# The first phase of a decoder block on one core: x by token halves, the first scaled half on VectorE, squares four tiles at a time

## The chip, the core and the metric

The kernel runs on one core of a Trainium2 chip. TensorE (PE) multiplies, VectorE (DVE), ScalarE (ACT) and GpSimd (POOL) do elementwise work, SyncE (SP) issues loads; each engine takes its instructions in its own order, and semaphores order the engines against each other. The metric is the device time in microseconds of one execution; the median of several runs is given.

## The reference

One layer of a decoder block over 512 tokens of 1024 channels, in float32:

```python
h = rmsnorm(x, norm1_g)
proj = h @ w_in            # columns: conv mixer, q, k and v of three branches, gates
y_a = a_b * causal_dwconv(a_c * a_x, conv_a_w)
y_b = nsa(q, compressed, selected and window keys, gates)
x = x + (gm_a * (y_a @ w_a_out) + gm_b * (y_b @ w_b_out)) @ w_o
h = rmsnorm(x, norm2_g)
x = x + (silu(causal_dwconv(h @ w_g) + b) * (h @ w_u)) @ w_down
```

where `rmsnorm(x, g) = x * rsqrt(mean(x*x) + eps) * g`. For this case only the first norm and the first part of `h @ w_in` matter: the 1048 token columns (q, keys, values, gates).

## The kernel before

x lies transposed in memory, as 8 tiles of 128 channels by 512 tokens (`KD` = 8). A float32 product is made of three products of a faster 32-bit format: a number is split into a high part `h` (a cast on ACT) and a rest `l` (a subtraction on DVE), and TensorE adds up h·h, h·l and l·h. The factor `rsqrt(mean(x*x))` of a token is a scale of a whole row, so it is left out of the products and applied when a result is read from its bank. x is only multiplied by the channel's gain `g`: `scale_x` makes `xg_h` (ACT) and `xg_l` (DVE).

The first phase (`tok_round`) makes the 1048 token columns of tokens 0 to 255 (two groups of 128, the tiles `pj_s`, `pj_t` and `pj_o`, six banks). It runs over k = 0 to 7. For each k, `on_k` scales x, loads the weight tile `wr_t` of k (512 KB), splits it (`wh_t` by ACT, `tok_lo` by DVE; the eight rests are kept for later), and adds the squares of x to `sq_sum` (a square on ACT, `square_x`, and an addition on DVE). TensorE then runs 18 products. x arrives in six loads of one or two whole tiles, in buffers of the tag `w4`, which all short-lived tiles of this phase share.

At k = 5 (`ROT_AT`) the tables of the rotary embedding are begun (`rotary_tables`), small steps on DVE, with two functions of ACT that each need a table load.

Behind the eight tiles, `row_scales` sums `sq_sum` over channels by eight short products into `pr`, and DVE (`ms`) and POOL (`r_n`) make the row factor of each token. `compress_in(0)` is a product of all of x with one weight tile (`wh_kc`, `wl_kc`, into `pkc`, 24 products of 512 columns). Then `tok_keep` casts weight tiles k = 0 to 3 again and keeps them (`th`, four buffers of the tag `th`), `compress_in(1)` is a second such product, and `tok_round_lag` makes the token columns of tokens 256 to 511, with the kept weights first and then with k = 4 to 7 loaded anew (`wr_t`, the first of them called t24 here). It writes to the same banks as the first phase, so it waits for `evac`: ACT reads three banks `pj_s` with the row factor, DVE the other three.

All raw weights, of the first phase, of `compress_in`, `tok_keep` and of the second round, go through three buffers of the tag `wr` (`NWR`), the split ones through two (`wh`). The order on each engine, and which buffer a tile gets, is chosen by the scheduler that builds the program; `behind` ties an instruction behind another by hand.

```python
raw = sb.tile([P, TOKC], F32, name=f"wr_th{k}", tag="wr", bufs=NWR)
h = th.tile([P, TOKC], F32R, name=f"th{k}", tag="th", bufs=LAG)
```

Of the kernel before, what the change touches and what calls it, by code (L numbers as in the profile page):

```python
# [11 lines left out]
F32 = mybir.dt.float32  # L12
F32R = mybir.dt.float32r
I32 = mybir.dt.int32
AF = mybir.ActivationFunctionType
ALU = mybir.AluOpType
AX = mybir.AxisListType

P = 128
D = 1024  # L20
S = 512
KD = D // P
# [20 lines left out]
TOKC = C_G + 24  # L43
# [5 lines left out]
ROT_AT = 5  # L49
LAG = 4  # L50

X_AT = {1: 1, 2: 2, 4: 2, 6: 1}
NWU = 9
QT_ORDER = (3, 2, 1, 0)
NPT = 3
NF_T = 10
# [13 lines left out]
CH = ((0, 350), (350, 700), (700, TOKC))  # L70

G1, G2, CAW, FCW, FCB = 0, 8, 16, 28, 94
# [17 lines left out]
def tile_block(ctx: ExitStack, tc: tile.TileContext, xT, pos, par, par2, w_tok, w_a3, w_gate, w_ao, w_bo, w_o,  # L90
               w_ff, w_dn, c_w1, out):
    nc = tc.nc
# [3 lines left out]
    pa = in_ctx.enter_context(tc.tile_pool(name="pa", bufs=1, side="left"))  # L96
    at_ctx = ExitStack()
    pb = at_ctx.enter_context(tc.tile_pool(name="pb", bufs=1, side="right"))
    pr_ctx = ExitStack()
    pp = pr_ctx.enter_context(tc.tile_pool(name="pp", bufs=1, side="right"))  # L100

    def const(shape, name, dt=F32, pool=sb):
        return pool.tile(shape, dt, name=name, tag=name)

    def w_tmp(name, shape):

        t = pp.tile([P, TOKC], F32, name=name, tag="w4", bufs=NW4)
        v = t[:, :math.prod(shape)]
        if len(shape) == 2:
            v = v.rearrange("p (a b) -> p a b", a=shape[0])  # L110
        elif len(shape) == 3:
            v = v.rearrange("p (a b c) -> p a b c", a=shape[0], b=shape[1])
        return v
# [4 lines left out]
    def d_bank(name):  # L118
        return bank("d", name, 2)
# [11 lines left out]
    loads, splits = [], []  # L131
# [30 lines left out]
    wu = d_bank("wu")  # L162
    for i in range(NWU):
        nc.tensor.matmul(wu[:, 0:P], ones, ones, start=True, stop=True)
    par_sb = const([P, NPAR], "par")
    xg_h = const([P, KD, S], "xg_h", F32R, pa)
    xg_l = const([P, KD, S], "xg_l", F32R, pa)
    sq_sum = w_tmp("sq_sum", (S,))


    def tok_banks(tt):
# [22 lines left out]
    def tok_round(tts, on_k):  # L194
        banks = [tok_banks(tt) for tt in tts]
        for k in range(KD):
            wh, wl = on_k(k, lambda first=0: load_w(w_tok[k], TOKC, f"t{tts[0]}{k}", first=first, mid=k > 0, lo=tok_lo_of(k)))
            for tt, bank in zip(tts, banks):
                tok_products(tt, bank, k, [wh[:, a:b] for a, b in CH], wl, k == 0, k == KD - 1)
        return banks  # L200
# [23 lines left out]
            tok_products(t1, banks[1], k, [kept[k][:, a:b] for a, b in CH], tok_lo_of(k), False, k == lag - 1)  # L224
        return banks

    def scale_x(k, xr, c):
        g = par_sb[:, G1 + k:G1 + k + 1]
        hi = nc.scalar.activation(xg_h[:, k, c], xr[:, c], AF.Copy, scale=g)
        nc.vector.scalar_tensor_tensor(xg_l[:, k, c], xr[:, c], g, xg_h[:, k, c].bitcast(F32),  # L230
                                       op0=ALU.mult, op1=ALU.subtract)
        return hi

    def square_x(k, xr, after):
        sq = sq_sum if k == 0 else w_tmp(f"sq{k}", (S,))
        behind(nc.scalar.activation(sq, xr, AF.Square), after)
        if k > 0:
            nc.vector.tensor_add(sq_sum, sq_sum, sq)

    xrs = {}  # L240

    def load_x(k, n):
        t = w_tmp(f"xr{k}", (n, S))
        for i in range(n):
            xrs[k + i] = t[:, i]
        nc.sync.dma_start(t, xT[:, k:k + n])

    def behind(later, earlier):

        tc.add_manual_dep(later.ins, earlier.ins.name,  # L250
                          mybir.DependencyInfo(mybir.DependencyClass.NoSync, mybir.DependencyReason.DATA),
                          reason="order")

    def on_k(k, load):
        if k == 0:

            load_x(0, 1)
            nc.sync.dma_start(par_sb, par)
            first, rest = slice(0, S // 2), slice(S // 2, S)
            scale_x(0, xrs[0], first)  # L260
            w = load(CH[0][1])
            load_x(1, 1)
            hi = scale_x(0, xrs[0], rest)
        else:
            hi = scale_x(k, xrs[k], slice(0, S))
            w = load(CH[0][1] if k == 1 else 0)
            if k in X_AT:
                load_x(k + 1, X_AT[k])
        square_x(k, xrs[k], splits[-1] if k < 2 else hi)
        if k == ROT_AT:  # L270

            for d in (nc.sync.dma_start(pos_i, pos), nc.sync.dma_start(par2_sb, par2)):
                behind(d, loads[-1])
            rotary_tables()
        return w


# [9 lines left out]
    def rotary_tables():  # L287
# [22 lines left out]
        for i, gi in enumerate((0, 2, 3)):  # L310
# [5 lines left out]
            nc.vector.tensor_tensor(tsin[:, i, :, HALF:], sn, glo, op=ALU.mult)  # L316

    banks0, banks1 = tok_round((0, 1), on_k)

    ident = const([P, P], "ident")  # L320
# [382 lines left out]
            nc.vector.scalar_tensor_tensor(mix_a[j], mix_a[j], 1.0, acc, op0=ALU.add, op1=ALU.mult)  # L703


    th_ctx = ExitStack()
    th = th_ctx.enter_context(tc.tile_pool(name="th", bufs=1, side="left"))
    compress_in(0)
    kept = [tok_keep(k) for k in range(2)]
    compress_in(1)  # L710
# [43 lines left out]
    half = D // 2  # L754
# [86 lines left out]
    for i in range(4):  # L841
# [6 lines left out]
        w = load_w(w_bo[i], D, f"bo{i}")  # L848
        for n, j in enumerate((2 * i, 2 * i + 1)):
# [7 lines left out]
                                           op0=ALU.mult, op1=ALU.subtract)  # L857
# [37 lines left out]
    for n, j in enumerate(order):  # L895
        w = load_w(w_o[j], D, f"o{j}")
# [6 lines left out]
        sq = sq2 if n == 0 else pc.tile([P, S], F32, name=f"sqb{j}", tag="tb", bufs=3)  # L903
# [208 lines left out]
```

## Time and profile before

| What | Value |
|---|---|
| median of 3 runs | 729.7 us (729.38 to 730.1) |
| span of the profiled execution, first to last instruction | 728.6 us |
| PE busy | 722.1 us, 99% |
| ACT busy | 416.8 us, 57% |
| bytes moved | 90.36 MB, 124 GB/s in the mean |
| granted clock of TensorE | 1.000 |

The profiled execution is recorded by its span, 728.6 us; a time of its own is not given, and the runs beside it are the three of the first row. In the profile, a row of the order of time has the start in us, the duration in us, the engine, the line, the operation, the tiles (written from read) and the count; in brackets stands how long the engine had been idle and what ended that. A row of a stage (a window) gives the length, then for PE, PE's weight load, DVE, ACT and POOL the busy time with the count, the granted clock, the share of the load engines and GB/s. PE's durations are modelled and overlap: the distance of two starts is what a product costs. Names in the profile lack the numbers of tiles.

### The profile page before, as it was taken

What the parts mean: (1) busy time and instruction counts of PE and PEld (TensorE: products, weight loads), DVE (VectorE), ACT (ScalarE), POOL (GpSimd) and SP (SyncE); (2) the same over time, 40 slices, a digit from 0 to 9 for tenths busy, and PEclk for the clock granted to TensorE, in tenths of its full rate; (3) what the DMA queues carried; (4) which work ended last, traced back from release to release, by engine and by line L of the source; (5) the groups of instructions that cost most, each with busy time, mean ns of one, the idle gap of its engine ahead of it and who ended that gap; (6) DMA issues with size and microseconds to landing.
All of it is one profiled execution on the core that took longest, in us unless ns stands there. A gap on an engine that the chain in (4) does not pass through costs nothing.

```text
span 728.6 us, 11253 instructions
## 1 busy us (share of the span) xinstructions
PE 722.1 (99%) x4315; PEld 641.7 (88%) x4315; DVE 568.2 (78%) x979; ACT 416.8 (57%) x697; POOL 122.7 (17%) x113
## 2 busy tenths in 40 slices
PE   8999999999999999999999999999999999999997
PEld 8999878888888888778889999999999999999986
DVE  6986966667556676688876989999898988989833
ACT  6866556758666676544666565555545564545320
POOL 2020334333333210322002010001000000000000
PEclk9999999999999999999999999999999999999999
DMA  8753551112111221245544686544655546552403
GB/s 289 243 167 109 150 140 60 57 62 83 58 59 58 75 70 58 72 160 173 195 138 107 142 186 165 159 127 115 152 141 142 145 117 155 135 144 88 117 29 116
DMA packets 36309, 90.36 MB, mean 124 GB/s; under 512 B 7456, under 2 KB 9120, under 8 KB 36256
## 3 DMA queue, kind: packets, MB, share of 16 engines
q1 hardware_dynamic: 30320, 76.75, 33.0%
q0 software_dynamic: 5648, 12.58, 10.4%
q8 instruction: 34, 0.56, 0.3%
q10 hardware_dynamic: 288, 0.31, 0.1%
q14 instruction: 19, 0.16, 0.1%
HBM read 87.54 MB, written 2.10 MB: 123 GB/s over the span
## 4 chain that ended last, share of the span: by engine, by line
PE 95%; DMA 3%; ACT 1%; DVE 0%; issue 0%; POOL 0%; SPq 0%; POOLq 0%
PE p L376 10%; PE p L372 10%; PE p L369 10%; PE pdn L369 4%; PE pdn L372 4%; PE pdn L376 4%; PE pg L369 4%; PE pg L374 4%; PE pg L372 4%; PE pa L369 3%; PE pa L372 3%; PE pt L623 2%; PE po L369 2%; PE po L372 2%; PE po L376 2%; PE pa L376 2%
## 5 line engine op out<-in xcount | busy, mean ns | idle before, releaser
L369 PE MATMUL p<-xf_h,sh 128*128 128x256 f32 x352 | 87.4, 281 | 0.0
L372 PE MATMUL p<-xf_l,sh 128*128 128x256 f32 x352 | 87.2, 281 | 0.0
L369 PEld LDWEIGHTS p<-xf_h,sh 128*128 128x128 f32 x352 | 66.3, 188 | 0.1
L372 PEld LDWEIGHTS p<-xf_l,sh 128*128 128x128 f32 x352 | 66.3, 188 | 0.0
L376 PE MATMUL p<-xf_h,sl 128*128 128x256 f32 x352 | 55.8, 281 | 0.0
L781 POOL DMA_DIRECT2D wl_d<-in_w_dn_dram x16 | 19.1, 1195 | 210.6 <-ACT wl_d L780 210.6
L758 ACT ACTIVATE sh<-s 128x1024 fp32r<-128x1024 f32 x44 | 45.8, 1051 | 15.1 <-DVE s L798 8.1
L759 DVE TENSOR_TENSOR sl<-s,sh 128x1024 fp32r<-128x1024 f32 x44 | 53.1, 1216 | 1.3 <-ACT sh L758 1.2
L372 PE MATMUL pdn<-al,wh_d 128*128 128x512 f32 x134 | 52.6, 393 | 0.0
L369 PE MATMUL pdn<-ah,wh_d 128*128 128x512 f32 x134 | 52.3, 392 | 0.0
L369 PE MATMUL pg<-xg_h,wh_g 128*128 128x512 f32 x128 | 51.0, 398 | 0.0
L372 PE MATMUL pg<-xg_l,wh_g 128*128 128x512 f32 x128 | 50.8, 397 | 0.0
L374 PE MATMUL pg<-xg_h,wl_g 128*128 128x512 f32 x128 | 50.7, 396 | 0.0
L376 PEld LDWEIGHTS p<-xf_h,sl 128*128 128x128 f32 x352 | 47.8, 188 | 0.2
L369 PE MATMUL p<-xf_h,wh_s 128*128 128x256 f32 x176 | 43.7, 281 | 0.0
L372 PE MATMUL p<-xf_l,wh_s 128*128 128x256 f32 x176 | 43.7, 281 | 0.0
L596 ACT ACTIVATE e<-sc,mx 128x256 f32<-128x256 f32 (+3 forms) x64 | 33.2, 524 | 13.0 <-DVE mx L595 11.6
L369 PE MATMUL pa<-xg_h,wh_a 128*128 128x512 f32 x96 | 38.5, 401 | 0.0
L372 PE MATMUL pa<-xg_l,wh_a 128*128 128x512 f32 x96 | 37.9, 395 | 0.0
L627 DVE TENSOR_TENSOR pl<-pt,ph 128x512 fp32r<-128x512 f32 x40 | 26.9, 683 | 13.7 <-ACT ph L626 13.6
L758 ACT ACTIVATE th<-wr_s 128x512 fp32r<-128x512 f32 x20 | 12.7, 634 | 39.5 <-issue 28.4
L600 ACT ACTIVATE e<-e,sums 128x512 f32<-128x512 f32 (+3 forms) x64 | 30.8, 552 | 7.6 <-DVE sums L574 7.6
(330 smaller groups left out, 2132.2 us busy)
## 6 DMA issues: line engine op xcount, KB each, us to landing
wr_s<-in_w_ff_dram SPq DMA_DIRECT2D x44, 512.0 KB, 3.5
wr_d<-in_w_dn_dram SPq DMA_DIRECT2D x22, 512.0 KB, 3.7
wr_g<-in_w_gate_dram SPq DMA_DIRECT2D x16, 512.0 KB, 3.4
wl_d<-in_w_dn_dram POOLq DMA_DIRECT2D x16, 512.0 KB, 6.4
wr_a<-in_w_a_dram SPq DMA_DIRECT2D x12, 512.0 KB, 3.5
wr_t<-in_w_tok_dram SPq DMA_DIRECT2D x10, 524.0 KB, 5.1
wr_o<-in_w_o_dram SPq DMA_DIRECT2D x8, 512.0 KB, 3.6
wr_th<-in_w_tok_dram SPq DMA_DIRECT2D x4, 524.0 KB, 3.9
```

What stands on the lines that cost most here:

```text
L369: m = nc.tensor.matmul(acc, wh, xh, start=first and i == 0, stop=False)
L372: nc.tensor.matmul(acc, wh, xl, start=False, stop=False)
L374: m = nc.tensor.matmul(acc, wl, xh, start=False, stop=last and i == n - 1)
L376: m = nc.tensor.matmul(acc, wl, xh, start=False, stop=last and i == n - 1)
L596: nc.scalar.activation(e[:, i, 0:nk], sc[:, o:o + nk], AF.Exp, bias=mx[:, i], accum_out=sums[:, i])
L600: nc.scalar.activation(v, v, AF.Copy, scale=sums[:, i])
L623: ends["pt"] = nc.tensor.transpose(pt[:, i * P:(i + 1) * P], e[:, i, kt * P:(kt + 1) * P], ident)
L627: nc.vector.tensor_sub(pl, pt, ph.bitcast(F32))
L758: nc.scalar.activation(h, v, AF.Copy)
L759: nc.vector.tensor_sub(l, v, h.bitcast(F32))
L781: nc.gpsimd.dma_start(view(l), src, accum_op=ALU.add)
```

## The change

x is loaded by token halves (`XH` = 256): tokens 0 to 255, which alone the first phase multiplies, in five loads that begin with single tiles, and tokens 256 to 511 in two loads of four tiles at k = 5 and k = 6. The halves lie in four tiles of the tag `th`, whose pool is opened earlier for it; the kept weights use the same four buffers afterwards. The very first scaled half is made by VectorE. The second half is scaled at k = 6 and 7. Squares are taken of four tiles of a half at once (1024 columns on ACT), and DVE adds the four by one reduction with a stride, so there are four squares, four reductions and two additions of 256 columns, where there were eight squares and seven additions of 512. `sq_sum` has a buffer of its own. The parameters come in two loads, and one of nine warming products is left out.

```diff
-X_AT = {1: 1, 2: 2, 4: 2, 6: 1}
-NWU = 9
+XH = 256
+NWU = 8
...
-    sq_sum = w_tmp("sq_sum", (S,))
+    sq_sum = const([P, S], "sq_sum", F32, pp)
...
-    def square_x(k, xr, after):
-        sq = sq_sum if k == 0 else w_tmp(f"sq{k}", (S,))
-        behind(nc.scalar.activation(sq, xr, AF.Square), after)
-        if k > 0:
-            nc.vector.tensor_add(sq_sum, sq_sum, sq)
...
+    def x_tile(half, q):
+        t = th.tile([P, TOKC], F32, name=f"xr{half}{q}", tag="th", bufs=LAG)
+        xrs[half, q] = t[:, 0:4 * XH].rearrange("p (k t) -> p k t", k=4)
+
+    def load_x(half, k, n):
+        if k % 4 == 0:
+            x_tile(half, k // 4)
+        return nc.sync.dma_start(xrs[half, k // 4][:, k % 4:k % 4 + n], xT[:, k:k + n, half * XH:(half + 1) * XH])
+
+    def scale_x(half, k, by_dve=False):
...
+        if by_dve:
+            hi = nc.vector.tensor_scalar(xg_h[:, k, c], xr, g, None, op0=ALU.mult)
+        else:
+            hi = nc.scalar.activation(xg_h[:, k, c], xr, AF.Copy, scale=g)
+        nc.vector.scalar_tensor_tensor(xg_l[:, k, c], xr, g, xg_h[:, k, c].bitcast(F32),
+                                       op0=ALU.mult, op1=ALU.subtract)
+        return hi
+
+    def square_x(half, q, after):
+        sq = w_tmp(f"sq{half}{q}", (4, XH))
+        behind(nc.scalar.activation(sq, xrs[half, q], AF.Square), after)
+        c = sq_sum[:, half * XH:(half + 1) * XH]
+        if q == 0:
+            nc.vector.tensor_reduce(c, sq.rearrange("p k t -> p t k"), axis=AX.X, op=ALU.add)
+        else:
+            part = w_tmp(f"sqp{half}", (XH,))
+            nc.vector.tensor_reduce(part, sq.rearrange("p k t -> p t k"), axis=AX.X, op=ALU.add)
+            nc.vector.tensor_add(c, c, part)
+
     def on_k(k, load):
         if k == 0:
...
+            load_x(0, 0, 1)
+            nc.sync.dma_start(par_sb[:, 0:CAW], par[:, 0:CAW])
+        hi = scale_x(0, k, by_dve=k == 0)
+        w = load(CH[0][1] if k < 2 else 0)
+        if k == 0:
+            load_x(0, 1, 1)
+        elif k == 1:
+            load_x(0, 2, 2)
+        elif k == 2:
+            load_x(0, 4, 4)
+        elif k == 3:
+            behind(nc.sync.dma_start(par_sb[:, CAW:], par[:, CAW:]), loads[-1])
+        elif k == 4:
+            square_x(0, 0, splits[-1])
         if k == ROT_AT:
...
+            behind(load_x(1, 0, 4), loads[-1])
             rotary_tables()
+        elif k == 6:
+            square_x(0, 1, splits[-1])
+            behind(load_x(1, 4, 4), loads[-1])
+            for j in range(4):
+                behind(scale_x(1, j), splits[-1])
+        elif k == 7:
+            square_x(1, 0, splits[-1])
+            square_x(1, 1, splits[-1])
+            for j in range(4, KD):
+                behind(scale_x(1, j), splits[-1])
         return w
```

What the scheduler makes of it, at the three places of which the prediction speaks. First, ACT around the end of the first phase, before the change (`wh_kc` is the cast for `compress_in`, `th` a kept weight, `qkv` the reading of a bank `pj_s`, `wh_t24` the cast of weight k = 4 of the second round):

```order
L147 ACTIVATE wh_kc0_431<-wr_kc0_430 128x1024
L208 ACTIVATE th0_472<-wr_th0_471 128x1048
L304 ACT_TABLE_LOAD
...
L208 ACTIVATE th1_476<-wr_th1_475 128x1048
L492 ACTIVATE qkv0_528<-pj_s00_95,r_n1_406 128x350
L492 ACTIVATE qkv0_528<-pj_s01_96,r_n1_406 128x350
L492 ACTIVATE qkv0_528<-pj_s02_97,r_n1_406 128x348
L147 ACTIVATE wh_kc1_480<-wr_kc1_479 128x1024
L505 ACTIVATE gate_n_422<-qkv0_528 128x24
L208 ACTIVATE th2_521<-wr_th2_520 128x1048
```

And the same place on ACT after the change:

```order
L149 ACTIVATE wh_kc0_437<-wr_kc0_436 128x1024
L210 ACTIVATE th0_478<-wr_th0_477 128x1048
L331 ACT_TABLE_LOAD
...
L210 ACTIVATE th1_482<-wr_th1_481 128x1048
L333 ACT_TABLE_LOAD
L333 ACTIVATE warm_75<-n_t_260 128x1
L149 ACTIVATE wh_kc1_486<-wr_kc1_485 128x1024
L210 ACTIVATE th2_527<-wr_th2_526 128x1048
L210 ACTIVATE th3_531<-wr_th3_530 128x1048
L149 ACTIVATE wh_t24_665<-wr_t24_664 128x1048
L519 ACTIVATE qkv0_534<-pj_s00_97,r_n1_415 128x350
```

The reading of the first bank stood behind the cast of th1; it stands behind the casts of kc1, th2, th3 and t24 now.

Second, SP's loads from th1 on with the semaphores that each waits for, before the change (DMAHW are earlier loads, DVE and Activation the engine that frees the buffer):

```order
L207 DMA wr_th1_475<-in_w_tok_dram 128x1048 [waits DMAHW6_49,DMAHW2_49,DVE_49]
L146 DMA wr_kc1_479<-in_w_a3_dram 128x1024 [waits DMAHW7_49,DMAHW5_49,Activation_49]
L207 DMA wr_th2_520<-in_w_tok_dram 128x1048 [waits DMAHW4_49,DMAHW0_49,DVE_49]
L207 DMA wr_th3_524<-in_w_tok_dram 128x1048 [waits DMAHW6_49,Activation_49]
L146 DMA wr_t24_658<-in_w_tok_dram 128x1048 [waits DMAHW0_49,Activation_49]
```

And after it:

```order
L209 DMA wr_th1_481<-in_w_tok_dram 128x1048 [waits DMAHW7_49,DMAHW4_49,DVE_49]
L148 DMA wr_kc1_485<-in_w_a3_dram 128x1024 [waits DMAHW6_49,DMAHW0_49,Activation_49]
L209 DMA wr_th2_526<-in_w_tok_dram 128x1048 [waits DMAHW7_49,DMAHW1_49,Activation_49]
L209 DMA wr_th3_530<-in_w_tok_dram 128x1048 [waits DMAHW5_49,DVE_49]
L148 DMA wr_t24_664<-in_w_tok_dram 128x1048 [waits DMAHW3_49,DMAHW1_49,Activation_49]
```

The order of the loads is the same, the buffers are not: th2 had the buffer of kc0 (freed by DVE's `wl_kc`) and has that of th1 now (freed by ACT's cast of th1); th3 has that of kc0. t24 has the buffer of th2 in both.

Third, DVE from its last weight tile of the phase to `wl_kc`, before (`ang` and `n_t` belong to the rotary table):

```order
L155 TENSOR_TENSOR tok_lo3_90<-wr_t07_352,wh_t07_353 128x1048
L299 SCALAR_TENSOR_TENSOR ang_273<-n_t_274,ang_273 128x128
L155 TENSOR_TENSOR wl_kc0_432<-wr_kc0_430,wh_kc0_431 128x1024
L300 TENSOR_SCALAR ang_273<-ang_273 128x128
L347 TENSOR_SCALAR ms_n1_404<-pr_n1_399 128x4
```

And after:

```order
L157 TENSOR_TENSOR tok_lo3_92<-wr_t07_348,wh_t07_349 128x1048
L264 TENSOR_REDUCE sq_sum_88<-sq10_353 128x256
L330 SCALAR_TENSOR_TENSOR n_t_260<-ang_259 128x128
L267 TENSOR_REDUCE sqp1_358<-sq11_356 128x256
L255 SCALAR_TENSOR_TENSOR xg_l_87<-xr11_318,par_85,xg_h_86 128x256 x4
L157 TENSOR_TENSOR wl_kc0_438<-wr_kc0_436,wh_kc0_437 128x1024
L268 TENSOR_TENSOR sq_sum_88<-sq_sum_88,sqp1_358 128x256
```

Between them stand now the two reductions and the four rests of the second half of x. On TensorE the row sums come in two pieces, of two token groups each, the second one behind all but two of the products `pkc`; the second round begins behind `pkc` in both programs.

More of the change, by code (lines that the diff above doesn't have):

```diff
@@ L98, in tile_block @@
     pb = at_ctx.enter_context(tc.tile_pool(name="pb", bufs=1, side="right"))
+    th_ctx = ExitStack()
+    th = th_ctx.enter_context(tc.tile_pool(name="th", bufs=1, side="left"))
     pr_ctx = ExitStack()
@@ L225, in tok_round_lag @@
         return banks
[L227 to L232, printed above, removed]
-    def square_x(k, xr, after):
-        sq = sq_sum if k == 0 else w_tmp(f"sq{k}", (S,))
-        behind(nc.scalar.activation(sq, xr, AF.Square), after)
-        if k > 0:
[L238 to L246, printed above, removed]
     def behind(later, earlier):
@@ L252, in behind @@
                           reason="order")
+    xrs = {}
+    def x_tile(half, q):
[6 more added lines that the diff above has]
+    def scale_x(half, k, by_dve=False):
+        g = par_sb[:, G1 + k:G1 + k + 1]
+        xr = xrs[half, k // 4][:, k % 4]
+        c = slice(half * XH, (half + 1) * XH)
+        if by_dve:
[5 more added lines that the diff above has]
+        return hi
@@ L254, in on_k @@
     def on_k(k, load):
         if k == 0:
[L257 to L269, printed above, removed]
+            load_x(0, 0, 1)
@@ L703, in mix_a_pair @@
             nc.vector.scalar_tensor_tensor(mix_a[j], mix_a[j], 1.0, acc, op0=ALU.add, op1=ALU.mult)
-    th_ctx = ExitStack()
-    th = th_ctx.enter_context(tc.tile_pool(name="th", bufs=1, side="left"))
     compress_in(0)
```

## The prediction

> **What bounds the kernel now.** I read the busy shares first, then the stages, then the waits of TensorE, and last the order of time on ACT, DVE and SP in the first 45 us, since the change lies there.
>
> ```profile
> PE 722.1 (99%) x4315; PEld 641.7 (88%) x4315; DVE 568.2 (78%) x979; ACT 416.8 (57%) x697; POOL 122.7 (17%) x113
> PE 95%; DMA 3%; ACT 1%; DVE 0%; issue 0%; POOL 0%; SPq 0%; POOLq 0%
> 73.00:243.00 170.00, 170.00 (x838) 140.83 (x837) 114.33 (x277) 111.84 (x241) 61.53 (x45) 1.00 0.28 81
> 243.00:390.00 147.00, 146.70 (x718) 121.56 (x717) 113.04 (x217) 87.88 (x176) 24.99 (x22) 1.00 0.36 117
> 390.00:715.00 325.00, 324.53 (x2296) 304.11 (x2295) 278.90 (x369) 165.20 (x202) 24.74 (x23) 1.00 0.51 131
> PE p L376 <- DMA wl_s<-in_w_ff_dram: 0.5, 1, 0.5
> PE ptc L616 <- DVE xs L613: 0.3, 1, 0.3
> ```
>
> TensorE sets the time: the chain is 95% PE, and from 73 us to 715 us it stands still for 0.8 us in all (two waits, which are the last two rows). So a stage behind the first one has no slack in which a delay could vanish, and a microsecond won or lost early arrives whole at the end. What counts is only when TensorE passes the last point that the change moves. TensorE's rows in the first phase, and its way out of it:
>
> ```profile
> 5.66 0.43 PE L186 MATMUL pj_s<-wh_t,xg_h 128*128 128x350 f32 x1 [0.50 <-ACT xg_h L229]
> 11.97 0.64 PE L186 MATMUL pj_s<-wh_t,xg_h 128*128 128x350 f32 x3
> 15.82 0.75 PE L186 MATMUL pj_s<-wh_t,xg_h 128*128 128x350 f32 x3 [0.56 <-ACT xg_h L229]
> 18.84 0.32 PE L186 MATMUL pj_s<-wh_t,xg_h 128*128 128x350 f32 x1
> 21.73 0.64 PE L186 MATMUL pj_s<-wh_t,xg_h 128*128 128x350 f32 x3
> 31.93 0.39 PE L374 MATMUL pkc<-xg_h,wl_kc 128*128 128x512 f32 x1
> 37.02 0.32 PE L186 MATMUL pj_s<-th,xg_h 128*128 128x350 f32 x1
> ```
>
> A channel tile is 18 products; the undisturbed one (k=4) takes 21.73 - 18.84 = 2.89 us. The one at k=2 takes 15.82 - 11.97 = 3.85, so 0.96 us is lost there to late x tiles. Phase two begins at 37.02, where the first product with a kept weight (th) writes bank s of the first round. That bank has to be emptied by ACT first. I measure the change at this instruction: behind it the two programs run the same work, in nearly the same order.
>
> **What emptied the bank in time.** ACT, SP and DVE around it:
>
> ```profile
> 28.61 1.08 ACT L208 ACTIVATE th<-wr_th 128x1048 fp32r<-128x1048 f32 x1 [0.15 <-DMA wr_th<-in_w_tok_dram]
> 33.03 1.07 ACT L208 ACTIVATE th<-wr_th 128x1048 fp32r<-128x1048 f32 x1
> 34.00 1.42 ACT L492 ACTIVATE qkv<-pj_s,r_n 128x350 f32<-128x350 f32 x3
> 41.95 1.08 ACT L147 ACTIVATE wh_t<-wr_t 128x1048 fp32r<-128x1048 f32 x1 [0.91 <-DMA wr_t<-in_w_tok_dram]
> 28.82 0.33 SPq L207 DMA_DIRECT2D wr_th<-in_w_tok_dram  x1
> 30.16 4.28 SPq L207 DMA_DIRECT2D wr_th<-in_w_tok_dram  x2
> 38.16 5.22 SPq L146 DMA_DIRECT2D wr_t<-in_w_tok_dram  x4
> 27.55 1.25 DVE L155 TENSOR_TENSOR tok_lo<-wr_t,wh_t 128x1048 fp32r<-128x1048 f32 x1
> 28.91 1.22 DVE L155 TENSOR_TENSOR wl_kc<-wr_kc,wh_kc 128x1024 fp32r<-128x1024 f32 x1
> ```
>
> The bank is read at 34.00, right behind the cast of th1 (33.03), and TensorE needs it at 37.02: 3 us to spare. The casts of th2, th3 and of the next weight (t24, at 41.95) come afterwards on ACT.
>
> **The change, the part that decides.** In the new order ACT reads the bank behind the casts of th2, th3 and t24. ACT works in order, so the bank now waits for their loads, and these hang in a chain: t24 goes into the buffer that the cast of th2 frees, and th2 into the one that the cast of th1 frees (SP's rows in the part on the change; before, th2 waited for wl_kc and was issued at 30.16, before th1 was cast). The rows for the sums, of loads (size, median us to landing) and of instructions (count, total us, mean ns):
>
> ```profile
> 25.33 3.82 SPq L207 DMA_DIRECT2D wr_th<-in_w_tok_dram  x2
> wr_t<-in_w_tok_dram SPq DMA_DIRECT2D x4, 524.0 KB, 4.3
> L492 ACT ACTIVATE qkv<-pj_s,r_n 128x350 f32<-128x350 f32 x2 | 1.0, 537 | 0.0
> L229 ACT ACTIVATE xg_h<-xr,par 128x512 fp32r<-128x512 f32 x7 | 5.0, 715 | 3.0 <-DMA xr<-in_xT_dram 3.0
> L229 ACT ACTIVATE xg_h<-xr,par 128x256 fp32r<-128x256 f32 x2 | 0.9, 492 | 0.0
> L236 ACT ACTIVATE sq<-xr 128x512 f32<-128x512 f32 x7 | 4.3, 615 | 0.0
> L230 DVE SCALAR_TENSOR_TENSOR xg_l<-xr,par,xg_h 128x512 fp32r<-128x512 f32 x7 | 5.2, 748 | 0.9 <-ACT xg_h L229 0.8
> L230 DVE SCALAR_TENSOR_TENSOR xg_l<-xr,par,xg_h 128x256 fp32r<-128x256 f32 x2 | 0.9, 481 | 0.0
> L238 DVE TENSOR_TENSOR sq_sum<-sq_sum,sq 128x512 f32<-128x512 f32 x7 | 4.8, 685 | 0.0
> L510 DVE TENSOR_REDUCE qst<-t 128x12 f32<-128x768 f32 x1 | 1.0, 955 | 0.0
> ```
>
> Step by step from the end of th1's cast:
> - load of th2, 3.6 us: between 3.28 (th0, issued 25.33, cast on landing at 28.61) and 3.79 (t24, issued 38.16, cast on landing at 41.95);
> - cast of th2, 1.07 (the th rows);
> - load of t24, 3.79 (its own row);
> - cast of t24, 0.97 to the next start (34.00 - 33.03);
> - one bank read, 0.54, and 0.05 to TensorE. Together 10.0 us.
>
> When does th1's cast end? Two things hold it. ACT's own work: I subtract about 0.1 from each duration, which the next instruction overlaps. The x work was 7 x 0.62 + 2 x 0.4 + 8 x 0.52 = 9.3 us; it becomes 15 halves x 0.41 plus four squares of 1024 columns. A square of 1024 is not in the trace; between twice 0.52 and the 0.97 of a 1048-column cast I take 1.0. That is 10.2 us, 0.9 more. Against that, ACT's 3.0 us of waits on xr may partly vanish, since only half of x is needed early. So the cast starts between 33.03 + 0.9 - 3.0 = 30.9 and 33.9; with a third of the waits staying, at 31.9, and it ends at 33.0. The other hold is th1's load, issued when DVE has split k=7. DVE's x work up to that point was 7 x 0.65 + 2 x 0.4 + 7 x 0.6 = 9.6 us. Now it is one multiply (0.3, near the 256-column row), 12 halves x 0.42, two reductions, one addition (0.35) and two small steps of the rotary table drawn forward (0.4). A reduction of four tiles reads 1024 elements with a stride; the nearest row takes 955 ns for 768 dense ones, so 1.2 us by elements, and twice that if the stride costs. At 1.2 the sum is 8.5, 1.1 less: k=7 is split at 28.7 - 1.1 - 0.5 for the earlier start = 27.1, th1 lands at 30.7, before ACT comes to it. ACT's own work decides.
>
> The bank is read, and TensorE goes on, at 33.0 + 10.0 = 43.0 instead of 37.02: **+6.0 us**. Bounds from the same rows: the cast's end from 32.0 to 35.0, the chain from 9.2 (both loads 3.28) to 11.2 (both 4.3, the wr_t row, with four loads queued); 41.2 to 46.2, or +4.2 to +9.2.
>
> **The parts that do not reach the end.** VectorE makes the first scaled half while ACT splits the first weight, and less data lies ahead: TensorE may begin some 0.6 us before 5.66, and the 0.96 us at k=2 and about 0.5 us in k=0 may go, 2.1 us in all. This ends in front of the wait for the bank and is worth nothing while that wait lasts. The same cover hides a second loss: behind k=7 DVE now does both reductions of the second half and its four split halves (1.2 + 0.2 + 1.2 + 1.7) before wl_kc, which is done at 27.1 + 4.3 + 1.15 = 32.6 instead of just before 31.93, so TensorE waits some 2 us at pkc too, after having arrived earlier. The second half of the row sums stands at the end of pkc, and its scale passes DVE and POOL before ACT may read the bank; all of it is done near 40 us, under the same wait. One warming product less, and the parameter load in two pieces, lie before 5.66 in time that waits for data. The new x buffers are the th buffers; a kept weight waits for readers of x that ACT has passed by then.
>
> The x rows that arrive now:
>
> ```profile
> xr<-in_xT_dram SPq DMA_DIRECT2D x4, 256.0 KB, 5.1
> xr<-in_xT_dram SPq DMA_DIRECT2D x2, 512.0 KB, 6.2
> ```
>
> A load of twice the size takes 1.2 times as long here, so a half should not cost as much as a whole. [...]
>
> **The rivals.**
> 1. *The loads do not decide.* If th1 is cast early and the loads overlap more than I read, a floor remains: t24's cast needs the buffer that the last pkc product reads, so bank and TensorE wait for one cast and one read behind it. wl_kc at 32.6, then 37.02 - 31.93 = 5.1 of pkc, 0.4 for the other half of the row sums, and 0.97 + 0.54 less the one product that still runs (0.23) plus hand-overs of 0.2: 39.6, +2.6, **732.3**. For it: the queue is nearly empty then. Against it: two loads cannot take less than 6.6 us in any row.
> 2. *Faster.* The early gain of 2.1 us survives, **727.6**. It needs the bank read by 34.4, so th1's cast ended by 34.4 - 0.97 - 3.79 - 1.07 - 3.28 = 25.3, earlier than k=7 is split today. The order would have to differ on the chip.
> 3. *The reductions cost double.* k=7 is split 2.4 us later, 29.5; th1 lands at 33.1 and its cast ends at 34.2, **736.9**.
> 4. *The halves bring nothing*, the x waits of 3.0 us all stay: cast's end at 35.0, **737.7**.
> 5. *All of it is hidden*, 729.7: only if 1 and 2 cancel.
>
> **The numbers.** The profiled execution spans 728.6 us, the median of the runs is 729.7; 1.1 us lies around the span, and I add the +6.0 to the median: **735.7**. Chances: the forecast (+4.2 to +7.0) 0.66, rival 1 0.14, rivals 3 and 4 0.13 together, faster 0.04, nothing 0.03. The range 732.8 to 738.4 takes in rivals 3 and 4 and stops above the middle of rival 1. A difference of 0.2% (1.5 us) is about what a measurement of this kernel can tell from none; faster 0.04, same 0.03, slower 0.93.
>
> **What would show it.** Right: a wait of TensorE for the bank's read by ACT (L519) of some 5 us, the first th product near 43, t24's cast directly ahead of the read and itself ended by its load, th2 issued at the end of th1's cast; a wait of some 2 us for wl_kc at L401; no new wait behind 73 us. Wrong: the bank read before 38, or th2 landing less than 3 us behind th1's cast, or a wait behind 73 us that before had not.

## The result, and the profile after

| What | Before | After |
|---|---|---|
| median, runs of one comparison | 729.90 us (4 runs, 729.38 to 731.05) | 740.16 us (4 runs, 739.12 to 740.35) |
| ratio, 95% interval | | 1.0136 (1.0124 to 1.0148) |
| span of the profiled execution | 728.6 us | 738.4 us |
| first product with a kept weight (th) | 37.02 us | 46.77 us |

The change costs 10.3 us. The forecast was 735.7 with a range up to 738.4: the direction held, the size did not.

The page of the changed kernel gives the busy shares and the chain of waits, as those rows were shown for before:

```profile
PE 724.9 (98%) x4313; PEld 643.1 (87%) x4313; DVE 573.9 (78%) x986; ACT 417.5 (57%) x699; POOL 124.2 (17%) x113
PE 92%; DMA 3%; DVE 2%; ACT 1%; issue 1%; SPq 0%; POOL 0%; ACTq 0%; POOLq 0%
```

TensorE still sets the time, with 92% of the chain instead of 95%. The late stages, each set some 11 us later than in the table of before, are unchanged:

```profile
84.00:254.00 170.00, 170.00 (x843) 141.02 (x841) 113.73 (x274) 111.83 (x241) 62.51 (x45) 1.00 0.25 79
254.00:401.00 147.00, 146.70 (x719) 121.65 (x718) 112.77 (x216) 87.45 (x176) 24.90 (x22) 1.00 0.35 117
401.00:725.00 324.00, 323.54 (x2287) 303.09 (x2286) 278.67 (x368) 164.69 (x201) 23.70 (x23) 1.00 0.50 131
```

So all of the loss lies in front of them: 46.77 - 37.02 = 9.75 us at the first th product, against 9.8 us at the end of the span. What TensorE waited for (us in all, times, longest), and its order of time up to there:

```profile
PE pkc L401 <- DVE wl_kc L157: 4.9, 1, 4.9
PE pj_s L188 <- ACT qkv L519: 1.5, 1, 1.5
PE pj_s L188 <- ACT wh_t L149: 0.7, 2, 0.4
PE pj_s L191 <- DVE tok_lo L157: 0.7, 1, 0.7
```

```profile
5.18 0.40 PE L188 MATMUL pj_s<-wh_t,xg_h 128*128 128x350 f32 x1 [0.33 <-DVE xg_h L252]
19.94 0.32 PE L188 MATMUL pj_s<-wh_t,xg_h 128*128 128x350 f32 x1
23.30 0.43 PE L188 MATMUL pj_s<-wh_t,xg_h 128*128 128x350 f32 x1 [0.33 <-ACT wh_t L149]
26.81 0.43 PE L188 MATMUL pj_s<-wh_t,xg_h 128*128 128x350 f32 x1 [0.38 <-ACT wh_t L149]
36.85 0.79 PE L401 MATMUL pkc<-xg_h,wl_kc 128*128 128x512 f32 x1 [4.86 <-DVE wl_kc L157]
44.92 0.40 PE L401 MATMUL pkc<-xg_h,wl_kc 128*128 128x512 f32 x1
46.77 0.43 PE L188 MATMUL pj_s<-th,xg_h 128*128 128x350 f32 x1 [1.46 <-ACT qkv L519]
```

The early gain is there: the first product comes at 5.18 instead of 5.66, and k = 5 begins at 19.94 instead of 21.73. Then it is lost. The wait for the bank, on which the forecast rested, is 1.46 us; the wait for `wl_kc`, which it held to be covered, is 4.86. Behind it the products themselves are slow: those of 512 columns start 0.43 us apart until 42.56, in the kernel before 0.23. The stages show it in the granted clock (third number from the end):

```profile
5.00:32.00 27.00, 25.41 (x150) 23.76 (x150) 22.91 (x38) 20.04 (x30) 0.59 (x2) 1.00 0.78 267
32.00:37.00 5.00, 0.15 (x1) 0.15 (x1) 5.00 (x9) 4.94 (x8) 0.00 (x0) 0.88 0.62 226
37.00:42.00 5.00, 5.00 (x12) 3.94 (x13) 3.83 (x15) 2.20 (x3) 0.00 (x0) 0.50 0.74 242
42.00:47.00 5.00, 3.54 (x16) 2.57 (x16) 0.99 (x3) 2.35 (x4) 1.84 (x3) 0.94 0.75 230
```

Between 37 and 42 us TensorE runs without a gap at a granted clock of 0.50. Before, it was 1.000 in the mean. Who made `wl_kc` late, and what held the bank, stands in the order of time on DVE, POOL, ACT and SP:

```profile
23.28 1.25 DVE L157 TENSOR_TENSOR tok_lo<-wr_t,wh_t 128x1048 fp32r<-128x1048 f32 x1 [1.29 <-ACT wh_t L149]
24.64 2.02 DVE L267 TENSOR_REDUCE sqp<-sq 128x256 f32<-128x1024 f32 x1
28.83 1.25 DVE L157 TENSOR_TENSOR tok_lo<-wr_t,wh_t 128x1048 fp32r<-128x1048 f32 x1
29.99 2.03 DVE L264 TENSOR_REDUCE sq_sum<-sq 128x256 f32<-128x1024 f32 x1
32.12 1.96 DVE L267 TENSOR_REDUCE sqp<-sq 128x256 f32<-128x1024 f32 x1
33.96 1.70 DVE L255 SCALAR_TENSOR_TENSOR xg_l<-xr,par,xg_h 128x256 fp32r<-128x256 f32 x4
35.54 1.25 DVE L157 TENSOR_TENSOR wl_kc<-wr_kc,wh_kc 128x1024 fp32r<-128x1024 f32 x1
44.78 0.16 DVE L374 TENSOR_SCALAR ms_n<-pr_n 128x4 f32<-128x4 f32 x1 [3.95 <-PE pr_n L371]
45.09 1.04 POOL L365 TENSOR_TENSOR r_n<-ms_n,mhalf 128x4 f32<-128x4 f32 x1 [39.45 <-DVE ms_n L374]
22.16 1.08 ACT L149 ACTIVATE wh_t<-wr_t 128x1048 fp32r<-128x1048 f32 x1 [3.80 <-DMA wr_t<-in_w_tok_dram]
33.99 1.06 ACT L210 ACTIVATE th<-wr_th 128x1048 fp32r<-128x1048 f32 x1
38.32 1.08 ACT L210 ACTIVATE th<-wr_th 128x1048 fp32r<-128x1048 f32 x1 [0.80 <-DMA wr_th<-in_w_tok_dram]
45.12 1.08 ACT L149 ACTIVATE wh_t<-wr_t 128x1048 fp32r<-128x1048 f32 x1 [2.65 <-PE pkc L399]
46.17 1.44 ACT L519 ACTIVATE qkv<-pj_s,r_n 128x350 f32<-128x350 f32 x3
35.08 2.07 SPq L209 DMA_DIRECT2D wr_th<-in_w_tok_dram  x2
```

DVE works through two reductions of 2.0 us and four scaled rests between the split of k = 7 (28.83) and `wl_kc` (35.54). At the other end two things finish almost together: at 46.13 the row factor `r_n` (45.09 + 1.04), whose last sums stand near the end of pkc, and at 46.2 (45.12 + 1.08) the cast of t24, which waits for pkc to let go of its buffer. ACT reads the bank right behind both. Neither waits for a load there.

The 9.75 us divide by the first `wl_kc` product: it comes 4.92 us later than before (36.85 - 31.93), and from it to the first th product are 9.92 us instead of 5.09.

### The profile page after: what moved, and what is told of

Read it like the earlier page. It is cut to its first block, busy times and chain, and to the rows that moved or that the text cites. A ratio compares the mean times of both kernels' runs of the same rounds, so it can differ in the third digit from the quotient of the medians.

```text
span 738.4 us, 11254 instructions
## 1 busy us (share of the span) xinstructions
PE 724.9 (98%) x4313; PEld 643.1 (87%) x4313; DVE 573.9 (78%) x986; ACT 417.5 (57%) x699; POOL 124.2 (17%) x113
## 4 chain that ended last, share of the span: by engine, by line
PE 92%; DMA 3%; DVE 2%; ACT 1%; issue 1%; SPq 0%; POOL 0%; ACTq 0%; POOLq 0%
PE p L403 10%; PE p L399 9%; PE p L396 9%; PE pdn L396 4%; PE pdn L399 4%; PE pdn L403 4%; PE pg L396 4%; PE pg L401 4%; PE pg L399 4%; PE pa L396 3%; PE pa L399 3%; PE pt L650 2%; PE po L396 2%; PE po L399 2%; PE po L403 2%; PE pa L403 2%
```

## The experiments

All kernels start from the changed one. Times are medians of 4 to 11 runs, each beside runs of the kernel before in the same comparison, and ratios are to that.

**1. The half sums behind `wl_kc`.** On DVE the two reductions of the second half, with their addition, go behind `wl_kc` (`late[2:]` are these reductions, `rests[-1]` the rest `wl_kc`).

```diff
     def compress_in(kv):
...
+        if kv == 0:
+            for m in late[2:]:
+                behind(m, rests[-1])
```

> The changed kernel with one order turned round on DVE: the two strided reductions and the addition for the second half of x stand behind wl_kc instead of in front of it. Nothing else in the first phase moves, but the reading of the bank by ACT then stands ahead of the cast of t24 (behind th3). Theory A (DVE's queue made the wait): wl_kc is ready 4.0 us earlier, near 32.8, TensorE's wait of 4.9 us at L401 shrinks to about 1 us, and the products pkc run at 0.24 us from start to start instead of 0.43, since the slow clock came from the wait. TensorE passes into the second round when ACT has cast th3 (landed at 41.39) and read the bank, near 43.0 instead of 46.8: 736.4 us. Theory B (what the prediction said: the chain of loads decides, whatever DVE does): the wait at L401 goes as well, but a wait for the bank of 4 us or more stands in its place, and the time is 737 to 740. If neither the reductions nor the queue matter, 740.2.

Measured: 737.39 us, 1.0099 (1.0080 to 1.0118), 2.8 us less. Its order of time on PE and POOL:

```profile
32.23 0.50 PE L401 MATMUL pkc<-xg_h,wl_kc 128*128 128x512 f32 x1 [1.10 <-DVE wl_kc L157]
38.18 0.61 PE L371 MATMUL pr_n<-ones,sq_sum 128*128 128x2 f32 x4 [0.59 <-DVE sq_sum L268]
41.98 0.43 PE L188 MATMUL pj_s<-th,xg_h 128*128 128x350 f32 x1 [3.20 <-ACT qkv L522]
40.30 1.04 POOL L365 TENSOR_TENSOR r_n<-ms_n,mhalf 128x4 f32<-128x4 f32 x1 [34.64 <-DVE ms_n L374]
```

The wait for `wl_kc` falls from 4.86 to 1.10, as theory A said, and the first th product comes 4.8 us earlier. Not all of it reaches the end: the span of the profiled execution is 3.9 us shorter (734.5 us), the median of the runs 2.8. The bank now waits for `r_n` alone (41.34), and TensorE stands still for 3.2 us; in the 5 us behind that its clock is 0.66. The median lies in the range of theory B, but the wait for the bank is not the one of theory B: it ends with the row factor and not with a load.

**2 and 3. The bank read ahead of the last two kept weights,** alone and together with 1: the cast of th2 goes behind the third read of `pj_s`.

```diff
+    behind(keeps[2], reads[2])
```

> The changed kernel with one order turned round on ACT: the bank's reading stands ahead of the casts of th2, th3 and t24. Theory A (the row factor r_n, behind the second half of the row sums at the end of pkc, is ready at 46.1 and would have held the read anyway): no change, 740.2 us within 0.4. Theory B (the casts and their loads held the bank): TensorE's wait of 1.5 us for the bank goes, 738.7 us.

> Both of the orders turned round: reductions behind wl_kc on DVE, bank read ahead of th2 on ACT. Theory A: wl_kc near 32.8, pkc at full clock and done near 38.5; the second half of the row sums comes when DVE has done reductions and addition, near 39, its factor r_n near 41, and TensorE goes on near 41.5 instead of 46.8: 735 us, that is 1.5 us less than with the first order alone. Theory B (loads): as with the first order alone, 736.4 or more.

Measured: 739.71 (1.0131, 1.0114 to 1.0148) and 737.91 (1.0110, 1.0094 to 1.0126): neither differs from its partner. The read no longer stands behind the casts of th2 and th3, nor behind their loads, and nothing is won. In read_first, on POOL and ACT:

```profile
43.76 1.04 POOL L365 TENSOR_TENSOR r_n<-ms_n,mhalf 128x4 f32<-128x4 f32 x1 [38.11 <-DVE ms_n L374]
43.78 1.08 ACT L149 ACTIVATE wh_t<-wr_t 128x1048 fp32r<-128x1048 f32 x1 [6.78 <-PE pkc L399]
44.84 1.44 ACT L521 ACTIVATE qkv<-pj_s,r_n 128x350 f32<-128x350 f32 x3
```

The read still comes when the row factor and t24's cast end, and both hang on the end of pkc. The chain of loads, the mechanism of the forecast, does not decide. The expectation of 735 for lo_read is a miss: it took the loads to hold the bank in lo_first.

**4 and 5. TensorE kept busy during the wait,** by 10 and by 20 products of ones into an unused part of the bank `pr`, between the second and the third pkc product. They add work and change no output (`firsts[0]` holds the second and the third pkc product).

```diff
+            if name == "n1" and t == 1:
+                for i in range(20):
+                    fill.append(nc.tensor.matmul(pr[:, 256:384], ones, ones, start=True, stop=True))
...
+        if kv == 0:
+            behind(fill[0], firsts[0][0])
+            behind(firsts[0][1], fill[-1])
```

> The changed kernel with ten products of ones (128 columns, 0.47 us each, into columns of pr that are written anew later) put where TensorE waits for wl_kc; all else in the first phase is as it was. Theory C (the halved clock from 36.9 to 42.3 is the answer to the idle 4.9 us): the granted clock stays at 1.00, the products pkc start 0.24 us apart instead of 0.43, pkc ends 2.5 us earlier, near 42.5, and the row factor near 43.7. How much of it arrives depends on t24's load, whose landing lies somewhere between 42.7 and 44.4: 737.7 to 739.4 us. If the slow clock has another cause, the rows stay 0.43 apart and the time is 740.2.

> As the run with ten products of ones, but with twenty, since a product of ones took 0.24 us there (20 rows in 2.39 us) and left 2.7 us of the wait empty: twenty last 4.8 us and fill it. Theory C (an idle TensorE of some microseconds is what halves the clock): the granted clock stays at 1.00 through pkc, its products start 0.24 us apart, pkc ends near 42.2, the row factor is ready near 43.4 and TensorE goes into the second round near 44: 737.5 us, 2.5 less than the changed kernel. If the slow clock does not come from the idle time, the rows stand 0.43 apart again and the time is 739.5 to 740.2.

Measured: 739.03 (1.0120, 1.0100 to 1.0140) with 10, which leave 2.69 us of the wait and a clock of 0.66 from 37 to 42; that one settles nothing. With 20: 736.45 (1.0086, 1.0069 to 1.0103). Rows of the order of time on PE and ACT, and one stage:

```profile
31.40 4.63 PE L377 MATMUL pr_n<-ones 128*128 128x128 f32 x40
36.49 0.50 PE L406 MATMUL pkc<-xg_h,wl_kc 128*128 128x512 f32 x1 [0.46 <-DVE wl_kc L157]
41.90 0.40 PE L406 MATMUL pkc<-xg_h,wl_kc 128*128 128x512 f32 x1
43.43 0.43 PE L188 MATMUL pj_s<-th,xg_h 128*128 128x350 f32 x1 [1.13 <-ACT qkv L528]
41.85 1.08 ACT L210 ACTIVATE th<-wr_th 128x1048 fp32r<-128x1048 f32 x1 [2.94 <-DMA wr_th<-in_w_tok_dram]
37.00:42.00 5.00, 5.00 (x25) 4.03 (x24) 3.77 (x15) 1.32 (x3) 1.31 (x3) 1.00 0.80 238
```

`wl_kc` is nearly as late as in the changed kernel (its product at 36.49 instead of 36.85), the clock stays at 1.00, and the time falls by 3.7 us. From the first product with `wl_kc` to the last are 5.41 us (36.49 to 41.90) instead of 8.07 (36.85 to 44.92): the slow clock cost 2.7 us. TensorE's wait for the bank is 0.3 us shorter too, but here other things moved with the fill: the builder put the second row sums further ahead within pkc, and ACT reads the bank behind the cast of th3, which waits 2.94 us for its load, and no longer behind that of t24. Neither bears on the clock: the idle 4.86 us of TensorE are what halved it here, since with that time filled, and `wl_kc` still late, it is 1.00 from 37 to 42 us instead of 0.50.

**6. Three mends at once:** 1, 2, and the row factor in two pieces, the first for tokens 0 to 255 alone.

```diff
+        for a, b in ((0, 2), (2, NT)) if name == "n1" else ((0, NT),):
...
+            rsqrt(r[:, a:b], ms[:, a:b], b - a)
```

> The changed kernel with three things undone: the reductions for the second half of x stand behind wl_kc, the row factor is made in two pieces (tokens 0 to 255 at once behind wl_kc, the others later), and ACT reads the bank ahead of the cast of th2. Theory A (behind wl_kc, the row factor at pkc's end is the only other thing that holds the bank): wl_kc near 33, pkc at full clock until 38.4, then the second row sums as soon as DVE has them (39.1), and the second round starts near 39.4 with the bank read long before, at 37.5: 46.8 - 39.4 = 7.4 us less, 732.8 us. Theory B (the loads of th1, th2 and t24 hold the bank or what follows): a wait of 3 us or more for a cast comes in its place, 735.5 to 737.

Measured: 736.83 (1.0092, 1.0071 to 1.0113). PE, ACT and the stage behind:

```profile
40.12 0.41 PE L188 MATMUL pj_s<-th,xg_h 128*128 128x350 f32 x1
43.17 1.64 PE L385 MATMUL pr_n<-dg_n,ones 128*128 128x128 f32 x8 [1.86 <-DVE dg_n L382]
42.00:47.00 5.00, 3.83 (x17) 3.83 (x18) 2.70 (x7) 1.53 (x4) 1.19 (x3) 0.67 0.90 303
```

The wait for the bank is gone and the first th product stands at 40.12, near the expected 39.4. It is given back behind it: the second piece of the row factor is now late for `dg_n`, TensorE waits 1.86 us, and its clock is slow again (0.67 from 42 to 47 us). So the time is 4.0 us above the expected 732.8. It lies in the range of theory B, but what waits is the row factor and not a cast.

**7. The second half of x one weight tile earlier,** and the second square of the first half at k = 5.

```diff
         elif k == 4:
             square_x(0, 0, splits[-1])
+            behind(load_x(1, 0, 4), loads[-1])
         if k == ROT_AT:
...
-            behind(load_x(1, 0, 4), loads[-1])
+            square_x(0, 1, splits[-1])
+            behind(load_x(1, 4, 4), loads[-1])
             rotary_tables()
         elif k == 6:
-            square_x(0, 1, splits[-1])
-            behind(load_x(1, 4, 4), loads[-1])
```

> The changed kernel with the second half of x loaded one weight tile earlier (ahead of t5 and t6 instead of t6 and t7) and the second square of the first half taken at k = 5. Nothing else is asked for; the second row sums come ahead of the first product with wl_kc in this order, so the row factor is early too. Expected if the two 512 KB loads ahead of t6 were what made t6 late (landed 22.16, four 2.0 us reductions still in DVE's queue): the waits of TensorE at k = 6 and 7 (1.4 us in all) go, wl_kc is ready near 35.2 instead of 36.7, TensorE still waits 4 to 5 us for it and then runs at half clock, and the second round starts near 43.4: 736.8 us. If the order of the loads does not matter, the waits at k = 6 and 7 stay and the time is above 738.

Measured: 735.98 (1.0081, 1.0066 to 1.0096), 4.2 us less than the changed kernel and near the expected 736.8, but not because the weight of k = 6 lands earlier: it is cast at 22.29, in the changed kernel at 22.16. What moved on DVE is the second reduction of the first half. It stands at 21.38, where DVE waits for that weight, and no longer between the splits of k = 6 and k = 7. The second row sums now stand ahead of `wl_kc`, and there is no wait for the bank. TensorE stands still for 3.66 us at these sums (34.83), and its mean clock from 37 to 42 us is 0.74.

**8. Dense additions in the place of the strided reductions,** at the same place.

```diff
-            nc.vector.tensor_reduce(c, sq.rearrange("p k t -> p t k"), axis=AX.X, op=ALU.add)
+            nc.vector.tensor_add(sq[:, 0:2], sq[:, 0:2], sq[:, 2:4])
+            nc.vector.tensor_add(c, sq[:, 0], sq[:, 1])
```

> The changed kernel with each strided reduction of four tiles replaced by two dense additions (512 and 256 columns), which stand at the same place on DVE, ahead of the rests of x and of wl_kc. Nearest rows: an addition of 512 columns took 0.69 us, one of 256 took 0.42, so 1.1 us where the reduction takes 2.02. Theory A (DVE's queue): three reductions ahead of wl_kc save 2.8 us in all, wl_kc is ready near 33.9, the wait at L401 shrinks to about 2 us; with the row factor made from sums that stand ahead of pkc's third product, the second round starts near 40 instead of 46.8: 733.3 us, up to 735 if the clock drops in the wait. If the stride costs nothing (the reductions take long for another reason), the additions take as long and the time stays near 740.

Measured: 736.45 (1.0088, 1.0072 to 1.0105). The two additions take 0.69 and 0.42 us against 2.02. The price of the reductions is not read from this run, because two more edges in its edit (not shown) hold the second half of x behind the squares, and the builder also moved a table load of ACT ahead of `wh_kc`. For that TensorE waits 2.51 us, and behind it the clock is 0.59 from 37 to 42 us, with products of 512 columns 0.43 us apart until 40.80.

**9 to 12. All mends together, and one part of the change put back in each of three others.** `mended` has the earlier x of 7, the dense additions, the row factor in two pieces, `wl_kc` ahead of the second half, the read ahead of th1, its table loads and sines behind that, and six buffers for short-lived tiles instead of five (`NW4`). Its main edges between instructions, beside the edits of 6, 7 and 8 without their own edges:

```diff
-NW4 = 5
+NW4 = 6
...
+        if kv == 0:
+            behind(squares[2], splits[-1])
+            for i in (4, 3, 2, 1):
+                behind(lows[-i], rests[-1])
+            behind(late[2], lows[-1])
...
+    behind(keeps[1], reads[2])
+    behind(sins[0], keeps[1])
...
+    behind(kc1_cast, reads[2])
```

> The changed kernel (x by halves, first scaled half on DVE, squares four at a time, all kept) with everything out of the way that the runs so far named: the second half of x loaded one weight tile earlier and the second square at k = 5; two or three dense additions in place of each strided reduction; wl_kc on DVE ahead of the last rests of x and of the second half's sums; those squares on ACT behind wh_kc; the row factor in two pieces; the bank read on ACT ahead of th1; the sine tables behind it; the spreading of the factor (pr rows) behind the third kept weight on TensorE; six buffers w4 instead of five. Theory A (DVE's queue, the row factor and the clock were all of the loss): wl_kc near 29.9, pkc done near 35.3, the second round starts at 35.5 to 36.0 instead of 37.02 in the kernel before, no clock below 1.00, and the early gain of 1.0 to 1.5 us arrives: 728.2 to 728.7 us. Theory B (the loads of th2, th3, t24 set the second round, whatever comes before): a wait for a cast of 2 us or more behind the start of the second round, 731 us or more.

The three others differ from it by one edit each: ScalarE makes the first scaled half, the strided reductions come back (the diff of 8 reversed), and the loads of x come at k = 5 and 6 again (the diff of 7 reversed for the loads).

```diff
-        hi = scale_x(0, k, by_dve=k == 0)
+        hi = scale_x(0, k)
```

> The mended kernel with the first scaled half made by ACT again, as in the kernel before. If the start is on the path there: the first product comes about 0.5 us later than in the mended one (5.66 in the kernel before against 5.18 in the changed one) and so does the end, +0.5 us. If a later wait sets the second round, no difference.

> The mended kernel with the strided reductions put back (2.02 us each for about 1.3 us of dense additions), at the same places. If a slow reduction costs only by what is queued behind it: the ones of the first half stand where DVE waits for t6, those of the second half behind wl_kc, where they delay only the second row sums, so 0 to +0.7 us on the mended kernel. [...]

> The mended kernel with the second half of x loaded at k = 5 and 6 again, as in the changed kernel. If the two 512 KB loads made t6 late: the waits of TensorE at k = 6 and 7 come back (1.4 us in the changed kernel), wl_kc is as much later, +1.4 us. If the order of the loads does not matter, within 0.3 us.

Measured: mended 744.53 (1.0198, 1.0182 to 1.0213), with the first half by ScalarE 744.97, with the reductions 745.94, with the later loads 743.44. These are misses by some 15 us, though the first th product came where it should. To mended the three others differ by +0.4, +1.4 and -1.1 us, where +0.5, then 0 to 0.7, and then +1.4 or none were expected; with the order below they say little of the parts. Of mended, on PE and by stage:

```profile
35.38 0.41 PE L189 MATMUL pj_s<-th,xg_h 128*128 128x350 f32 x1
86.23 0.90 PE L589 MATMUL pqt<-ident,t 128*128 128x128 f32 x6 [3.59 <-DVE t L577]
87.00:92.00 5.00, 3.12 (x13) 2.36 (x12) 3.23 (x7) 2.85 (x8) 1.82 (x2) 0.50 0.57 104
92.00:97.00 5.00, 2.05 (x4) 1.16 (x4) 4.53 (x15) 2.81 (x9) 0.56 (x1) 0.50 0.00 0
```

The second round begins 1.64 us earlier than before; at the first product of the conv mixer (`pa`) 0.25 us of that are left (71.23 against 71.48). Then TensorE comes to the transpositions of the second round (`pqt`) after two of its weight tiles instead of three, and has to wait for VectorE, at half clock through both stages shown.

**13 to 16. The same with five buffers,** by which the order of TensorE from 71 us on is that of before.

```diff
-NW4 = 6
+NW4 = 5
```

> The kernel mended, with five buffers for short-lived tiles as in the changed kernel, where mended had six. Theory A (mended lost its time behind 81 us only because the sixth buffer let the builder put the transpositions of the second round two weight tiles of the conv mixer earlier, where TensorE then waits and its clock halves): the first th product stays near 35.4 us against 37.02 before, TensorE has no wait over 1 us behind it, the granted clock is 1.00, and the time is 728.3 us (727.6 to 729.2), 1.6 us under the kernel before. Theory B (the mends themselves postpone work of VectorE that is missing later): waits for DVE t stay, and the time is 732 or more.

> As mended5, with the very first scaled half made by ScalarE again. In mended and its twin the first th product moved from 35.38 to 35.76 us by this. Theory A: 0.4 us more than mended5, 728.7 us. Theory B: like mended5, since the later waits decide.

> As mended5, with the four strided reductions put back in the place of the dense additions. In mended and its twin the first th product moved from 35.38 to 35.89 us by this. Theory A: 0.5 us more than mended5, 728.8 us. If the strided reductions alone were the fault of the change, it would be 3 us or more.

> As mended5, with the loads of x for tokens 256 to 511 one weight tile later again, at k = 5 and 6 as in the changed kernel. In mended and its twin the first th product moved from 35.38 to 36.23 us by this. Theory A: 0.85 us more than mended5, 729.1 us. If the place of these loads were the fault of the change, it would be 3 us or more.

| Kernel | Median | Ratio to before (95%) |
|---|---|---|
| mended5 | 730.52 | 1.0011 (1.0002 to 1.0020) |
| mended5_act (first half by ScalarE) | 730.15 | 1.0004 (0.9995 to 1.0013) |
| mended5_late (x loads as in the change) | 730.64 | 1.0010 (1.0001 to 1.0019) |
| mended5_red (strided reductions) | 732.81 | 1.0049 (1.0037 to 1.0062) |

Theory A holds in its main point: no wait over 1 us is left behind the first phase in mended5, the clock is 1.00, and 14 us are won back with the buffer's number alone. It misses by 2.2 us. The first th product stands at 36.50 in the profiled execution instead of 35.38. There the weight of k = 6 was cast at 23.42 instead of 22.29; in mended5_act, with the same five buffers, it was cast at 21.83 and that product stands at 35.78, so the number of buffers does not account for it. With five buffers the reading of the bank waits until DVE has added the squares, th1 and th2 come later, and TensorE waits 0.79 us for th2. What takes the rest stays open: in mended5_act the first th product is 1.24 us earlier than before, the first `pa` product 0.15 (71.33). Two rows of mended5 and two of mended5_red (ACT and PE, in this order):

```profile
34.11 1.44 ACT L541 ACTIVATE qkv<-pj_s,r_n 128x350 f32<-128x350 f32 x3 [1.64 <-DVE sq_sum L273]
40.41 0.43 PE L189 MATMUL pj_s<-th,xg_h 128*128 128x350 f32 x1 [0.79 <-ACT th L214]
```

```profile
35.17 1.44 ACT L541 ACTIVATE qkv<-pj_s,r_n 128x350 f32<-128x350 f32 x3 [4.48 <-DVE sqp L275]
41.46 0.43 PE L189 MATMUL pj_s<-th,xg_h 128*128 128x350 f32 x1 [2.13 <-ACT th L214]
```

With the strided reductions that hold is 4.48 us, the next kept weights are cast later, and TensorE waits 2.13 us: 2.3 us more in the median, between the 0.5 and the 3 us of its two expectations. The first half by VectorE and the place of the loads of x change nothing that can be told apart. No kernel tried beats the one before; the best, mended5_act, equals it.

## Why the prediction was wrong in size

**TensorE has no slack behind the first phase: right.** 9.75 us at the first th product, 9.8 at the end of the span. That is shown for a loss only: of what mended5_act gains at that product, 0.15 of 1.24 us is left at the first `pa` product.

**The bank wait by the chain of loads: the step that failed.** The prediction put the bank read at 43.0 by the loads of th2 and t24. The order on the engines was read rightly: th2 was issued (35.08) when th1's cast ended (33.99 + 1.06), and ACT read the bank behind t24's cast. But t24's cast waited for TensorE (pkc), not for its load, and read_first, which frees the read of th2 and th3 with their loads, wins nothing. The chain's own parts were near: with th1's cast ending at 35.05, at the upper end of the bounds given, the 10.0 us behind it would have let TensorE go on at 45.05. It went on at 46.77. That the two are near each other is chance, since the read did not wait for that chain. The measured +10.3 us also lies above the prediction's own upper bound of +9.2, where its range stopped at 738.4.

**"wl_kc, which is done at 32.6 ... all of it is done near 40 us, under the same wait": here lies the missing time.** `wl_kc` was done at 36.7, and the wait priced at some 2 us was 4.86. Of the 4.1 us, 2.9 were lost by the end of the split of k = 7 (29.99 instead of 27.1), and what lay behind it took 1.25 more. There are two causes. The prediction summed DVE's work from the start to the split of k = 7 and credited 1.1 us less of it, and 0.5 for the earlier start. But the split of k = 6 waits for its weight: ACT stood idle for 3.80 us until it landed, DVE for 1.29, and the split began at 23.28 whatever had been saved ahead. From there to the end of the split of k = 7 are 6.71 us, in which DVE also does one reduction, an addition and four rests of x. Why that weight landed late was not settled; in mended5_late the place of the loads of x makes no difference. The other cause is the size of a reduction: the sum took a strided one at 1.2 us, by its elements, and named twice that as the other end. Measured are 2.02, nearer to that end; from start to start the three at 24.64, 29.99 and 32.12 take 1.94, 1.93 and 1.84, 2.1 us more than 3 x 1.2, one third of it ahead of the split of k = 7. Moving two of them away (lo_first) takes the wait from 4.86 to 1.10; putting all four into the otherwise mended kernel costs 2.3 us. Rival 3 had this price, but charged it to th1's load and found 736.9. The reductions read one element of each 1 KB and took 2.02 us, against 1.25 for a dense `wl_kc` of as many elements. A reduction as such is not so dear: the prediction's own row has a dense one of 768 elements at 0.955 us. Whether the stride costs it, or the many sums of only four elements, was not told apart.

**What such a wait does was left out of the sum.** The forecast treated a wait of TensorE as lost time and no more. The trace of before has no wait over 1.1 us and a clock of 1.000, so it could not show what the changed kernel's shows, a clock of 0.50 behind one of 4.86 us. This cost 2.7 us, as warm2 shows, and it stretched pkc, at whose end the row factor and t24's cast hang. With that the 9.75 us come together: 4.92 by the wait and what led to it, 2.66 by the clock, 1.62 between the last pkc product and the first th product (1.85 instead of 0.23), and 0.55 that pkc took besides, with the second row sums in it.

**Rival 1's floor came true.** Its rule was that bank and TensorE wait, behind pkc, for one cast and one read: first `wl_kc` product plus 5.1 + 0.4 + 1.5. From the measured 36.85 that gives 43.8, and with 2.7 us of slow clock 46.5; measured 46.77. It had the right mechanism and 14% of the chance, and the forecast's own `wl_kc` time made it look harmless at 39.6.

**The gain in front: right, and worth nothing, as said.** TensorE begins 0.48 us earlier and is 1.8 us ahead at k = 5. mended5_act shows that even in a kernel without the loss the new first half on VectorE adds nothing.

## What to carry to other kernels

A loss that is said to lie under another wait has to be worked out as carefully as that wait, with its dear bound too: here the covered one was the dearer. When TensorE is the bound, price a wait of some microseconds at its length plus what the slower clock behind it may cost (here 4.86 and 2.7 us), and look first at whether something harmless can keep it busy. A buffer count or an edge in one phase can reorder products fifty microseconds later, so a mend is judged by the whole time and not by the stage it mends.

## What the runs showed of the hardware

The granted clock of TensorE fell behind idle times of 4.86 us (after: 0.50 from 37 to 42 us), 3.66 (early: 0.74 from 37 to 42, products 0.43 us apart until 39.40), 3.20 (lo_first: 0.66 from 42 to 47), 2.69 (warm: 0.66 from 37 to 42), 2.51 (dense2: 0.59 from 37 to 42, products 0.43 us apart until 40.80) and 1.86 us (fix, at the end of a broken stretch: 0.67 from 42 to 47). In the changed kernel it was at 0.50 for 5.7 us of work, from 36.85 to about 42.5, with products of 512 columns 0.43 us apart instead of 0.23; in warm for some 3 us. After an idle time of 2.13 us in mended5_red the stage from 42 to 45 us shows a clock of 1.00:

```profile
42.00:45.00 3.00, 3.00 (x22) 2.82 (x21) 1.81 (x5) 2.99 (x8) 0.00 (x0) 1.00 0.68 190
```

So the length of one gap alone does not decide: the clock fell behind 1.86 us in fix and stood at 1.00 behind 2.13 us here. What else decides was not tried.
